# Attention operands of a head pair split when the pair's first head begins, with zero-padded low parts, another order in block 1 and other figures in the planner

## The chip, the core and the metric

The kernel runs on one core of a Trainium2 chip. The metric is the device time of one execution in microseconds. TensorE multiplies; VectorE (DVE), ScalarE (ACT) and GpSimd (POOL) do the elementwise work; the queue of SyncE (SP) carries most of the loads from device memory.

## The reference, cut to what matters

Three model blocks run one after the other on one sequence of 512 tokens of width 1024, all in float32:

```
x = first_block(x, c, ctx, c_ctx, ...)   # gated linear attention (4 heads) + depthwise conv (31 taps)
                                         # + spatial gating unit, three gates, then a feed-forward
x = second_block(x, ...)                 # 2 layers: feed-forward, hybrid mixer, feed-forward
x = third_block(x, c_3, ...)             # linear recurrence + block attention of 8 heads
```

Three things in it matter here. In block 1 the output is `gates0*y_a + gates1*y_b + gates2*y_c`, where `y_a` is the product of the gated linear attention (GLA), `y_b` that of the convolution and `y_c` that of the spatial gating unit, and every gate is a sigmoid of a projection of the same input. In each layer of block 2 the mixer has 8 softmax heads with a forget bias ("Fox", 64 features, in 4 pairs) and 4 differential heads ("Diff") of two 64-feature softmaxes each:

```
s_f = einsum('bhqd,bhkd->bhqk', qf, k_f) * scale + cf[..., None] - cum[..., None, :]
s_d = einsum('bhcqd,bhckd->bhcqk', qd, k_d) * scale
```

Block 3 has 8 causal softmax heads of 64 features (for 512 tokens its block selection keeps every past block), again in 4 pairs ("Moba").

## The kernel before

All large products run in a rounded float32 format with both operands split in a high and a low part, as three matmuls (`mm3`): weight high by input high, weight high by input low, weight low by input high. 24 of them (8 blocks of the contraction by 3) are a "unit" of 128 output columns by 512 tokens. Weights come as a stream of [128,1024] pieces, three in flight: SP loads `wraw`, ACT casts it to `whi`, and DVE (or POOL, for every second piece where `poolprep` is set) subtracts to get `wlo`.

Everything else is written as generators ("tasks") that are advanced after each `mm3` (`main_mm3`, then `tick`). The order of instructions on every engine is thus made when the program is built, by a planner: `Clock` adds up a cost for each instruction (`cost_pe`, `cost_act`, `cost_dve`, `cost_pool`), and `yield from k.sync()` holds a task back until the planned time of TensorE has reached the planned end of what the task waits for. On the chip TensorE takes its instructions in that order; where a planned time was too short, it waits. `room(n)` holds a task until n of the 78 [128,512] blocks of on-chip memory are free, and `idle()` advances the planner with no main matmul.

Attention works on pairs of heads of 64 features. `stack` makes the operands of a pair from a block `t` with both heads: for each head `e` of the queries a block `out[e]` with the high part on the head's own 64 partitions and the low part on the other 64; for the keys a block with the high part on both halves, and one block `low` for both heads that holds the low parts. `attn_scores` then makes each block of 128 queries by two matmuls: one over all 128 partitions (high and low query by high key), and one over the head's own 64 partitions (high query by low key). Three parts of a head (`PARTS`) cover its four query blocks: 512 key columns, 384, and two times 256.

Fox: `fox(j)` projects queries and keys of pair j, and starts a task `prep` for each that runs `stack` at once; a head is `ready` when both are stacked. Moba: `head_norms` ends with `stack` for each pair, all four of the queries ahead of the keys. Diff heads run `stack` in their own `prelude`, as they begin. At most four heads are live at a time (`HEADS`, `H3`), in the order in which they were started. The mixer ends in `out_proj`: a first pass over the Diff results, and a second one that needs the Fox results.

Block 1 begins with 8 loads of `x`, 8 of the first group of modulation weights (`ada.load(0)`), 3 weight pieces and 8 more of group 1, all on SP. `warm(7)` runs matmuls on zeros; sums of squares, `rms_cols` (row norms), `ada.rows(0)` and two calls of `prepare` follow, and then the first main matmuls. Later the units follow `ORDER_1`: "r" are gates of the GLA output, "g" the gates of a branch, "p" a product with a branch's output, which waits until all 8 blocks of that output are there, "a" starts the modulation rest, "v" and "s" belong to the spatial gating unit. The convolution (`conv_work`, 240 fused multiply-adds on DVE) is a filler that is advanced when DVE's planned queue is short.

Of the kernel before, what the change touches and what calls it, by code (L numbers as in the profile page):

```python
# [18 lines left out]
S = 512  # L19
SC = 256  # L20
KT = 8
# [202 lines left out]
def cost_dve(op, out, a, kw):  # L224
    n = width(out)
    if op == "reciprocal":
        return 0.07 + 6.4e-3 * n
    if op in ("tensor_scalar", "memset"):
        return max(0.2, 0.1 + 0.7e-3 * n)
    return max(0.2, 0.08 + 1.05e-3 * n)  # L230


def cost_pool(op, out, a, kw):
    return 0.06 + (1.0e-3 if op == "memset" else 2.3e-3) * width(out)


class Engine:
# [532 lines left out]
def stack(k, t, keys):  # L770


    nc = k.nc
    yield from k.sync()
    yield from k.room(4)
    out = [k.rblk(), k.rblk()]
    low = k.rblk() if keys else None
    own = [slice(0, 64), slice(64, 128)]
    for e in range(2):
        nc.scalar.copy(out[e].r[own[e]], t.f[own[e]])  # L780
    if keys:
        for e in range(2):
            nc.scalar.copy(out[e].r[own[1 - e]], t.f[own[e]])
    yield from k.sync()
    for e in range(2):
        lo = (low.r if keys else out[e].r)[own[e] if keys else own[1 - e]]
        nc.gpsimd.tensor_sub(lo, t.f[own[e]], out[e].f[own[e]])
    k.free(t)
    if keys:
        out.append(low)  # L790
    return out


def attn_scores(k, q, kk, e, part):
    b = k.bank()
    rows = slice(64 * e, 64 * e + 64)
    for qb, o in part:
        n, c = max((qb + 1) * P, 256), slice(qb * P, qb * P + P)
        k.nc.tensor.matmul(b[:, o:o + n], lhsT=q[e].r[:, c], rhs=kk[e].r[:, 0:n], start=True, stop=False)
        k.nc.tensor.matmul(b[:, o:o + n], lhsT=q[e].r[rows, c], rhs=kk[2].r[rows, 0:n], start=False, stop=True)  # L800
    return b


# [88 lines left out]
class Pair:  # L892

    nb = 1
    whole = True

    def turned(self, i):

# [89 lines left out]
class Fox(Pair):  # L988
# [8 lines left out]

    def prelude(self):
        k, nc, st = self.k, self.k.nc, self.st
        self.q, self.kk, self.v = st["q"][self.j], st["k"][self.j], st["v"]  # L1000
        yield from k.room(4)
        self.ncum, self.nmd, self.sm = k.blk(), k.blk(), k.tiny()
        b = yield from k.gbank()
        sel = k.negr[0:40, self.h:self.h + 1].to_broadcast([40, P])
        nc.tensor.matmul(b, lhsT=sel, rhs=st["cum"].r[0:40], start=True, stop=True)
        yield from k.sync()
        nc.scalar.copy(self.ncum.f, b)
        k.unbank(b)
        tri = k.c("mask")[:, None, 384:512].to_broadcast([P, 4, P])
        v = lambda ap: ap.rearrange("p (b q) -> p b q", q=P)  # L1010
        nc.gpsimd.tensor_add(v(self.nmd.f), v(self.ncum.f), tri)
# [170 lines left out]
def mixer2(k, layer, norm, start, add, done):  # L1182
    nc = k.nc
    w = "w_in_2"
    xs = norm.xs
    st = dict(q={}, k={}, dq={}, dk={}, t={}, o={}, do={}, done=[0] * 4, ddone=[])
    st["nlam"], st["subln"] = k.lam[layer]
    k.poolprep = True
    pf = k.bank()
# [46 lines left out]
            k.free(cosr)  # L1236
        k.start(attn_head(k, Diff(k, st, h), HEADS))

    def prep(name, j, t):
        yield from k.sync()  # L1240
        st[name][j] = yield from stack(k, t, name == "k")

    def fox(j):
        for name, base, s in (("q", FQ, 0.125), ("k", FK, 1.0)):
            b = k.bank()
            k.unit(b, w, layer, base + j * P, xs)
            t = k.blk()
            nc.vector.scalar_tensor_tensor(t.f, b, s, norm.bc, op0=ALU.mult, op1=ALU.mult)
            k.unbank(b)
            k.start(prep(name, j, t))  # L1250
        for e in range(2):
            k.start(attn_head(k, Fox(k, st, j, e), HEADS))

# [326 lines left out]
class Moba(Pair):  # L1580
# [6 lines left out]
        return self.j in self.st["ga"] and self.j in self.st["q"] and self.j in self.st["k"]  # L1587

    def prelude(self):
        self.q, self.kk = self.st["q"][self.j], self.st["k"][self.j]  # L1590
        self.sm = self.k.tiny()
        self.k.clk.t = self.k.clk.now + 1.0
        yield from self.k.sync()

    def reduce(self, qb, o, bs, ss):
        n = qb * P + P
# [6 lines left out]
def head_norms(k, banks, g, keys, dst):  # L1603

    nc = k.nc
    heads = lambda ap: ap.rearrange("p (h d) -> p h d", d=64)
    yield from k.sync()
    ts = []
    for b in banks:
        yield from k.room(2)  # L1610
        ts.append(k.blk())
        nc.scalar.copy(ts[-1].f, b)
        k.unbank(b)
        yield
    st = k.blk()
    v, y, u = (st.f[:, 32 * i:32 * i + 32] for i in range(3))
    yield from k.sync()
    for i, t in enumerate(ts):
        yield from k.room(2)
        sq = k.blk()  # L1620
        k.act(sq.f, t.f, AF.Square)
        yield from k.sync()
        nc.vector.tensor_reduce(out=v[:, 8 * i:8 * i + 8], in_=heads(sq.f), axis=mybir.AxisListType.X, op=ALU.add)
        k.free(sq)
    nc.vector.tensor_scalar(v, v, 1.0 / 64, EPS1, op0=ALU.mult, op1=ALU.add)
    k.rsqrt(y, v, u)
    for i, t in enumerate(ts):
        eng = nc.gpsimd if i % 2 else nc.vector
        eng.tensor_mul(heads(t.f), heads(t.f), y[:, 8 * i:8 * i + 8, None].to_broadcast([P, 8, 64]))
    k.free(st)  # L1630
    yield from k.sync()

    def pair(j):
        yield from k.wait(2)
        yield from k.room(3)
        b = k.bank()
        for i, t in enumerate(ts):
            nc.tensor.transpose(b[:, i * P:i * P + P], t.f[:, j * P:j * P + P], k.ident)
        yield from k.sync()
        t = k.blk()  # L1640
        k.act(t.f, b, AF.Copy, scale=g)
        k.unbank(b)
        yield from k.sync()
        dst[j] = yield from stack(k, t, keys)
    for j in range(4):
        k.start(pair(j))
        yield
    while len(dst) < 4:
        yield
    k.free(ts)  # L1650
# [78 lines left out]
def block3(k, x, norm, out):  # L1729
    nc = k.nc  # L1730
    w = "w_in_3"
    st = dict(q={}, k={}, t={}, o={}, ga={}, done=[0] * 4)
    k.poolprep = True
    bs = k.nbanks(4)
    for t, p in enumerate(norm.each()):
# [133 lines left out]
def between(b, ahead):  # L1869

    o = []
    for m in range(KT):
        o += some("p", [m], b)
        if m + ahead < KT:
# [1 line left out]
    return o  # L1876


ORDER_1 = (some("r", range(KT)) + some("g", range(6), 1) + some("g", range(6), 0) + between(1, 6) + some("a", [0])
           + between(0, 6) + some("v", range(2)) + some("s", range(KT)) + some("g", range(6), 2) + between(2, 6))  # L1880


def plan1():
# [75 lines left out]
class Ada1:  # L1959
# [20 lines left out]
    def rows(self, q):  # L1980

        k, nc = self.k, self.k.nc
        b, row = k.bank(), k.blk()
        for t in range(KT):
            nc.tensor.matmul(b[0:2], lhsT=self.sc[:, t, :], rhs=self.ws[q][t].f, start=t == 0, stop=t == KT - 1)
        nc.scalar.copy(row.f[0:2], b[0:2])
        k.unbank(b)
        b = k.bank()
        for i in range(4):
            nc.tensor.transpose(b[:, 2 * i:2 * i + 2], row.f[0:2, i * P:i * P + P], k.ident[0:2, 0:2])  # L1990
        for c in range(2):
            self.finish(q, c, b[:, c:8:2])
        k.unbank(b)
        k.free(row, self.ws.pop(q))

    def step(self, q, c, t, acc):
        ve, w, s = self.k.nc.vector, self.ws[q][t].f, self.sc[:, t, c:c + 1]
# [91 lines left out]
def gla_dir(k, st, h, s, res):  # L2089
# [48 lines left out]
                         start=True, stop=True)  # L2138
    pairs = lambda ap: ap.rearrange("p (b c t) -> p b c t", c=2, t=64)
    chunk = dec.rearrange("p (b c) -> p b c", c=2)  # L2140
    nc.gpsimd.tensor_mul(both, chunk[:, :, 0], chunk[:, :, 1])
    f, l = pairs(kd.f)[:, :, s], pairs(qe.f)[:, :, 1 - s]
    nc.gpsimd.tensor_mul(f, f, chunk[:, :, 1 - s:2 - s].to_broadcast([P, 4, 64]))
    nc.gpsimd.tensor_mul(l, l, chunk[:, :, s:s + 1].to_broadcast([P, 4, 64]))
# [284 lines left out]
def block1(k, x, nxt):  # L2429
    nc = k.nc  # L2430
    w = "w_in"
    st = dict(q={}, k={}, v={}, r={}, o={}, ck={}, cv={}, s0=[k.blk() for _ in range(4)], cdone=0, hdone=0,
              conv={}, hc={}, yb={}, z={}, sv={})
    for m in range(KT):
        x.append(k.blk())
        nc.sync.dma_start(x[m].f, k.a["x"][:, m, :])
    ada = Ada1(k)
    ada.load(0)
    k.w_start()
    ada.load(1)  # L2440
    warm(k, 7)
    k.clk.t = k.clk.c["dve"] = k.clk.c["act"] = 6.0
    acc = sumsq(k, [x[m].f for m in range(KT)], S, nc.vector)
    lt, ly = rms_cols(k, acc.f, S, EPS1)
    ada.rows(0)
    bcb = bc_rows(k, ly)
    hx = []

# [7 lines left out]
        k.free(x[m])  # L2456

    prepare(0)
    k.w_ensure(1)
    k.w_finish(1)  # L2460
    prepare(1)
    ada.load(2)
    cols = k.bank()
# [4 lines left out]
    for m in range(KT):  # L2468
        q = m // 2 + 1
        if m % 2 == 0 and q < 4:  # L2470
            k.fresh()
            for t in range(KT):
                ada.step(q, 0, t, gacc)
            summed = k.clk.t
        for n, c0 in enumerate(first_units()):
            k.main_mm3(fb[n], k.wnext(w, 0, m, c0), (hx[m][0].r, hx[m][1].r), m == 0, m == KT - 1)
            if m % 2 == 1 and n == 1 and q < 4:
                k.clk.t = summed
                ada.sums(cols[:, 4 * q:4 * q + 4], gacc)
                ada.finish(q, 0, cols[:, 4 * q:4 * q + 4])  # L2480
                for i in range(2):
                    prepare(m + 1 + i)
        if m == 0:
            ada.load(3)
        elif m == 2:
            for i in range(4):
                nc.scalar.dma_start(cq[i].f.rearrange("p (m t) -> p m t", t=SC), k.a["ctx"][:, 2 * i:2 * i + 2, :])
# [338 lines left out]
```

## Time and profile before

| what | value |
|---|---|
| time, median of 3 runs | 3515.91 us (3515.6 to 3515.91) |
| the profiled execution's own time | 3511.07 us |
| its span, first to last instruction | 3509.3 us |
| busy TensorE | 3405.3 us, 97% of the span |
| busy DVE / ACT / POOL | 1911.7 / 1351.7 / 720.5 us |
| mean granted TensorE clock | 0.98 |

The profiled execution is 1.8 us longer than its span and 4.8 us shorter than the median of the runs. A matmul counts as busy from its start to its modelled end, and the next one starts before that end; how long matmuls take in a row is therefore read from the starts of successive rows, not from the durations. In shapes, `128*128 128x512` are weights of 128 partitions by 128 columns and a moving operand of 128 partitions by 512 columns; `64*128` are weights on 64 partitions.

### The profile page before, as it was taken

Reading aid. Unit: us, or ns where it says so; the run is one execution under the profiler, and the core shown is the slowest. Engines: PE = TensorE matmul, PEld = TensorE weight load, DVE = VectorE, ACT = ScalarE, POOL = GpSimd, SP = SyncE. Lnnn points to the kernel's source line nnn. Section 1 sums busy time; section 2 is a strip of 40 time slices with the busy share of each in tenths; the row PEclk is TensorE's granted clock in tenths of the full one; section 3 lists DMA queues with packets and bytes.
Section 4 is the critical chain, followed back from the end, with each engine's and each line's share of the span. In section 5 each row is a group of like instructions: output and inputs, shape, how many; then the busy total and the mean of one; then the engine's idle time right before and its main releaser. Section 6 shows DMA issues by size and latency. Waiting matters only on the chain.

```text
span 3509.3 us, 39437 instructions
## 1 busy us (share of the span) xinstructions
PE 3405.3 (97%) x15210; PEld 2763.3 (79%) x15210; DVE 1911.7 (54%) x3010; ACT 1351.7 (39%) x2176; POOL 720.5 (21%) x564
## 2 busy tenths in 40 slices
PE   7998889999999999999999999999999999999999
PEld 5886678887888888887778888888887778888777
DVE  5899865655333365433686443344335774433566
ACT  3324462223322332324764222233227653232474
POOL 0004231222000101103452110011016331111362
PEclk9998999999999999999999999999999999999999
DMA  6211114543322244232122222322332123222221
GB/s 209 93 56 55 48 49 149 181 156 102 102 98 99 99 159 164 97 117 98 55 68 80 99 97 96 96 96 97 107 108 72 60 68 108 96 96 96 72 79 55
DMA packets 110189, 344.99 MB, mean 98 GB/s; under 512 B 13425, under 2 KB 13681, under 8 KB 110001
## 3 DMA queue, kind: packets, MB, share of 16 engines
q1 hardware_dynamic: 84960, 296.78, 25.2%
q10 hardware_dynamic: 23760, 41.50, 3.7%
q0 software_dynamic: 1280, 4.20, 0.4%
q8 instruction: 119, 1.95, 0.2%
q14 instruction: 70, 0.57, 0.1%
HBM read 336.13 MB, written 6.29 MB: 98 GB/s over the span
## 4 chain that ended last, share of the span: by engine, by line
PE 52%; DVE 4%; ACT 2%; POOL 1%; issue 1%; DVEq 0%; POOLq 0%; ACTq 0%
PE bk L256 52%; DVE b L256 3%; ACT b L256 1%; DVE tinies L256 1%; POOL b L256 1%; POOL wlo L256 0%; DVE wlo L256 0%; ACT whi L256 0%; ACT L251 0%; ACT bk L256 0%; ACT tinies L256 0%; DVE small L256 0%; DVEq L256 0%; POOLq L256 0%; ACTq L256 0%
## 5 line engine op out<-in xcount | busy, mean ns | idle before, releaser
L256 PE MATMUL bk<-b,whi 128*128 128x512 f32 (+1 forms) x8048 | 2514.7, 394 | 6.8 <-ACT whi L256 3.4
L256 PEld LDWEIGHTS bk<-b,whi 128*128 128x128 f32 x8048 | 1506.7, 190 | 323.3 <-issue 9.6
L256 PE MATMUL bk<-b,wlo 128*128 128x512 f32 (+1 forms) x4024 | 1575.4, 391 | 6.7 <-DVE wlo L256 5.9
L256 POOL TENSOR_TENSOR b<-b,b 128x512 f32<-128x512 f32 (+2 forms) x381 | 528.4, 1395 | 2391.1 <-DVE b L256 1189.4
L256 DVE TENSOR_TENSOR wlo<-wraw,whi 128x1024 fp32r<-128x1024 f32 x495 | 643.8, 1303 | 528.8 <-ACT whi L256 528.5
L256 PEld LDWEIGHTS bk<-b,wlo 128*128 128x128 f32 x4024 | 762.2, 189 | 170.1 <-DVE wlo L256 8.8
L256 ACT CAST whi<-wraw 128x1024 fp32r<-128x1024 f32 x542 | 568.0, 1049 | 739.8 <-PE bk L256 442.8
L256 ACT CAST b<-b 128x512 fp32r<-128x512 f32 (+3 forms) x286 | 176.0, 618 | 523.9 <-POOL b L256 369.9
L256 DVE TENSOR_TENSOR b<-bk,b 128x512 f32<-128x512 f32 (+6 forms) x324 | 208.1, 659 | 253.7 <-PE bk L256 212.9
L256 DVE TENSOR_TENSOR b<-b,b 128x512 fp32r<-128x512 f32 (+3 forms) x250 | 184.7, 745 | 251.0 <-ACT b L256 248.9
L256 PE MATMUL bk<-b,b 128*128 128x128 f32 (+9 forms) x1056 | 250.4, 354 | 33.2 <-POOL b L256 20.4
L256 ACT ACTIVATE b<-b 128x512 f32<-128x512 f32 (+1 forms) x259 | 153.4, 608 | 308.7 <-DVE b L256 273.1
L256 PEld LDWEIGHTS bk<-b,b 128*128 128x128 f32 (+3 forms) x1056 | 174.1, 193 | 109.9 <-issue 36.0
L256 PE MATMUL bk<-whi,b 128*128 128x512 f32 x768 | 248.4, 397 | 4.0 <-ACT b L256 2.2
L256 DVE SCALAR_TENSOR_TENSOR b<-b,pvt,b 128x392 f32<-128x392 f32 (+7 forms) x296 | 229.0, 778 | 33.3 <-ACT b L256 26.4
L256 PEld LDWEIGHTS bk<-whi,b 128*128 128x128 f32 x768 | 145.6, 190 | 36.6 <-DVE b L256 3.0
L256 DVE SCALAR_TENSOR_TENSOR b<-b,small,b 128x512 f32<-128x512 f32 (+1 forms) x178 | 148.0, 833 | 20.8 <-ACT b L256 15.5
L256 POOL TENSOR_TENSOR wlo<-wraw,whi 128x1024 fp32r<-128x1024 f32 x47 | 116.0, 2467 | 202.3 <-ACT whi L256 175.7
L256 PE MATMUL bk<-wlo,b 128*128 128x512 f32 x384 | 150.8, 393 | 0.0
L256 PE MATMUL bk<-cst,b 128*128 128x128 f32 (+1 forms) x776 | 111.5, 271 | 36.3 <-DVE b L256 25.3
L256 PEld LDWEIGHTS bk<-cst,b 128*128 128x128 f32 x776 | 98.9, 168 | 60.4 <-DVE b L256 31.8
L256 ACT ACTIVATE b<-bk 128x512 f32<-128x512 f32 (+2 forms) x170 | 97.2, 572 | 111.6 <-PE bk L256 109.9
(93 smaller groups left out, 1233.9 us busy)
## 6 DMA issues: line engine op xcount, KB each, us to landing
wraw<-in_wst SPq DMA_DIRECT2D x542, 512.0 KB, 3.3
b<-in_ada1r ACTq DMA_DIRECT2D x64, 256.0 KB, 4.4
b<-in_ada ACTq DMA_DIRECT2D x48, 256.0 KB, 4.1
b<-in_ada SPq DMA_DIRECT2D x32, 256.0 KB, 5.5
xpark<-b ACTq DMA_DIRECT2D x16, 256.0 KB, 2.0
b<-xpark POOLq DMA_DIRECT2D x16, 256.0 KB, 5.2
b<-in_x SPq DMA_DIRECT2D x8, 256.0 KB, 5.2
b<-in_x ACTq DMA_DIRECT2D x8, 256.0 KB, 4.5
```

What stands on the lines that cost most here:

```text
L256: return f(*a, **kw)
```

## The change

`stack` makes one low block for each head of the keys, and ACT writes zeros (copied from a zero column of `mask`) to the half of it that is not the head's own. The second matmul of `attn_scores` runs over all 128 partitions. Fox and Moba keep `t`, and the pair's first head stacks queries and keys in its `prelude`; the second head waits for that. In block 1 the order of the start, `ORDER_1` and the engine of one small product are changed, and three planner costs.

```diff
 def cost_dve:
+    if op == "tensor_tensor_scan":
+        return 0.03 + 2.2e-3 * n
+    if op == "scalar_tensor_tensor" and n > 300 and len(tuple(out.shape)) == 3:
+        return 0.2 + 1.1e-3 * n
 def cost_pool:
-    return 0.06 + (1.0e-3 if op == "memset" else 2.3e-3) * width(out)
+    return 0.06 + 1.0e-3 * width(out) if op == "memset" else max(0.5, 0.1 + 2.7e-3 * width(out))
 def stack:
-    yield from k.room(4)
+    yield from k.room(5 if keys else 4)
-    low = k.rblk() if keys else None
+    lows = [k.rblk(), k.rblk()] if keys else out
...
             nc.scalar.copy(out[e].r[own[1 - e]], t.f[own[e]])
+            nc.scalar.copy(lows[e].r[own[1 - e]], k.c("mask")[own[1 - e], 0:1].to_broadcast([64, S]))
...
-        lo = (low.r if keys else out[e].r)[own[e] if keys else own[1 - e]]
-        nc.gpsimd.tensor_sub(lo, t.f[own[e]], out[e].f[own[e]])
+        nc.gpsimd.tensor_sub(lows[e].r[own[e] if keys else own[1 - e]], t.f[own[e]], out[e].f[own[e]])
 def attn_scores:
-        k.nc.tensor.matmul(b[:, o:o + n], lhsT=q[e].r[rows, c], rhs=kk[2].r[rows, 0:n], start=False, stop=True)
+        k.nc.tensor.matmul(b[:, o:o + n], lhsT=q[e].r[:, c], rhs=kk[2 + e].r[:, 0:n], start=False, stop=True)
 class Pair:
+    def stacks(self):
+        k, st, j = self.k, self.st, self.j
+        if j not in st["stk"]:
+            st["stk"][j] = None
+            qk = {}
+            def part(name):
+                qk[name] = yield from stack(k, st[name][j], name == "k")
+            yield from both_of(k, [part("q"), part("k")])
+            st["stk"][j] = qk["q"], qk["k"]
+        while st["stk"][j] is None:
+            yield
+        self.q, self.kk = st["stk"][j]
 Fox.prelude:
+        yield from self.stacks()
 fox(j):
-            k.start(prep(name, j, t))
+            st[name][j] = t
 Moba.prelude:
-        self.k.clk.t = self.k.clk.now + 1.0
-        yield from self.k.sync()
+        yield from self.stacks()
 head_norms:
-        dst[j] = yield from stack(k, t, keys)
+        dst[j] = t
-ORDER_1 = (some("r", range(KT)) + some("g", range(6), 1) + some("g", range(6), 0) + between(1, 6) + some("a", [0])
-           + between(0, 6) + some("v", range(2)) + some("s", range(KT)) + some("g", range(6), 2) + between(2, 6))
+ORDER_1 = (some("r", range(KT)) + some("g", range(KT), 0) + some("g", range(KT), 1) + some("a", [0]) + between(0, KT)
+           + between(1, KT) + some("v", range(2)) + some("s", range(KT)) + some("g", range(6), 2) + between(2, 6))
 gla_dir:
-    nc.gpsimd.tensor_mul(both, chunk[:, :, 0], chunk[:, :, 1])
+    nc.vector.tensor_mul(both, chunk[:, :, 0], chunk[:, :, 1])
 block1:
+    ada = Ada1(k)
+    ada.load(0)
     for m in range(KT):
         x.append(k.blk())
         nc.sync.dma_start(x[m].f, k.a["x"][:, m, :])
-    ada = Ada1(k)
-    ada.load(0)
+    k.w_start(1)
+    ada.load(1)
     k.w_start()
-    ada.load(1)
-    warm(k, 7)
+    row = ada.rows(0)
+    warm(k, 3)
...
-    ada.rows(0)
+    ada.turn(0, row)
+    k.w_ensure(0)
+    k.w_finish(0)
+    warm(k, 3)
     bcb = bc_rows(k, ly)
...
     prepare(0)
-    k.w_ensure(1)
-    k.w_finish(1)
     prepare(1)
...
-            if m % 2 == 1 and n == 1 and q < 4:
+            if m % 2 == 1 and n == 3 and q < 4:
```

`ada.rows` is cut in two: `rows` runs the matmuls, and the new `turn` copies, transposes and finishes. With `between(0, KT)` the eight products of a branch follow one another with no gate unit among them.

## Rows read from the trace of the kernel before

**Rows 1.** Stretches: from:to, length, busy (instructions) of PE, PEld, DVE, ACT, POOL; PEclk, DMA

```profile
1100.00:1150.00 50.00, 50.00 (x222) 41.40 (x221) 18.00 (x17) 14.65 (x18) 2.58 (x2) 1.00 0.28 95
263.00:508.00 245.00, 204.68 (x947) 164.72 (x948) 211.76 (x293) 127.16 (x248) 94.75 (x83) 0.90 0.15 50
1650.00:1863.00 213.00, 206.16 (x903) 152.28 (x902) 155.71 (x420) 143.78 (x333) 106.92 (x88) 0.95 0.19 65
2660.00:2874.00 214.00, 208.28 (x922) 155.36 (x922) 157.15 (x421) 141.98 (x333) 107.81 (x89) 0.96 0.20 66
3390.00:3483.00 93.00, 87.89 (x400) 65.34 (x399) 63.98 (x171) 63.29 (x133) 33.73 (x35) 0.96 0.14 46
```

**Rows 2.** TensorE's groups by shape: count, busy us, mean ns, idle before, releasers

```profile
L256 PE MATMUL bk<-b,b 64*128 64x256 f32 x80 | 31.9, 398 | 0.0
L256 PE MATMUL bk<-b,b 64*128 64x512 f32 x40 | 20.1, 503 | 8.4 <-POOL b L256 8.4
L256 PE MATMUL bk<-b,b 64*128 64x384 f32 x40 | 18.8, 470 | 0.0
```

**Rows 3.** Timeline of TensorE in Diff heads: start, length, operation, count; scores are `bk<-b,b`

```profile
1722.02 2.55 PE L256 MATMUL bk<-b,b 128*128 128x256 f32 x8
1724.50 0.50 PE L256 MATMUL bk<-whi,b 128*128 128x512 f32 x1
1724.84 0.39 PE L256 MATMUL bk<-wlo,b 128*128 128x512 f32 x1
...
1728.39 1.67 PE L256 MATMUL bk<-b,b 128*128 128x512 f32 x4
1729.99 0.50 PE L256 MATMUL bk<-whi,b 128*128 128x512 f32 x1
```

**Rows 4.** Groups by shape on ACT and POOL: `stack`'s casts and subtractions, `gla_dir`'s `both`

```profile
L256 ACT CAST b<-b 64x512 fp32r<-64x512 f32 x120 | 74.0, 616 | 4.1 <-POOL b L256 1.9 <-DVE b L256 0.2
...
L256 POOL TENSOR_TENSOR b<-b,b 64x512 fp32r<-64x512 f32 x80 | 109.6, 1370 | 43.1 <-ACT b L256 36.3 <-issue 2.0
...
L256 POOL TENSOR_TENSOR tinies<-tinies 128x4 f32<-128x4 f32 x8 | 5.6, 705 | 0.0
```

**Rows 5.** Timeline of TensorE where block 3's first Moba head begins

```profile
3396.78 0.79 PE L256 MATMUL bk<-b,b 64*128 64x512 f32 x1 [4.88 <-POOL b L256]
```

**Rows 6.** TensorE's waits from 263 to 508 us: total us, times, longest

```profile
PE bk L256 <- POOL b L256: 19.3, 10, 3.3
PE bk L256 <- DVE b L256: 16.9, 4, 7.9
```

**Rows 7.** Timelines of POOL and DVE: three taps beside POOL's five operations, four later

```profile
336.92 8.30 POOL L256 TENSOR_TENSOR b<-b,b 128x512 f32<-128x512 f32 x5 [7.78 <-DVE b L256]
...
342.35 5.04 DVE L256 SCALAR_TENSOR_TENSOR b<-b,pvt,b 128x480 f32<-128x480 f32 x3
...
370.89 2.70 DVE L256 SCALAR_TENSOR_TENSOR b<-b,pvt,b 128x424 f32<-128x424 f32 x4
```

**Rows 8.** TensorE's main groups to 519.5 us, and GLA's last transposes (timeline)

```profile
L256 PE MATMUL bk<-b,whi 128*128 128x512 f32 (+1 forms) x830 | 264.6, 403 | 3.4 <-ACT whi L256 3.4
...
L256 PE MATMUL bk<-whi,b 128*128 128x512 f32 x192 | 59.4, 389 | 0.0
...
519.57 0.60 PE L256 MATMUL bk<-cst,b 128*128 128x128 f32 x4
```

**Rows 9.** Timeline of the start

```profile
6.61 4.26 ACT L256 ACTIVATE b<-b 128x512 f32<-128x512 f32 x8
...
7.40 8.56 PE L256 MATMUL bk<-b 128*128 128x512 f32 x14 [7.40 <-DVE b L256]
...
16.67 7.03 PE L256 MATMUL bk<-b,small 128*2 128x512 f32 x16
...
29.26 1.22 PE L256 MATMUL bk<-b,whi 128*128 128x512 f32 x2 [3.41 <-ACT whi L256]
...
40.59 1.87 PE L256 MATMUL bk<-cst,b 128*128 128x1 f32 x8 [3.84 <-DVE b L256]
```

More of the change, by code (lines that the diff above doesn't have):

```diff
@@ L783, in stack @@
             nc.scalar.copy(out[e].r[own[1 - e]], t.f[own[e]])
+            nc.scalar.copy(lows[e].r[own[1 - e]], k.c("mask")[own[1 - e], 0:1].to_broadcast([64, S]))
     yield from k.sync()
     for e in range(2):
-        lo = (low.r if keys else out[e].r)[own[e] if keys else own[1 - e]]
-        nc.gpsimd.tensor_sub(lo, t.f[own[e]], out[e].f[own[e]])
+        nc.gpsimd.tensor_sub(lows[e].r[own[e] if keys else own[1 - e]], t.f[own[e]], out[e].f[own[e]])
     k.free(t)
-    if keys:
-        out.append(low)
-    return out
+    return out + lows if keys else out
 def attn_scores(k, q, kk, e, part):
     b = k.bank()
-    rows = slice(64 * e, 64 * e + 64)
     for qb, o in part:
@@ L999, in prelude @@
         k, nc, st = self.k, self.k.nc, self.st
-        self.q, self.kk, self.v = st["q"][self.j], st["k"][self.j], st["v"]
+        self.v = st["v"]
+        yield from self.stacks()
         yield from k.room(4)
@@ L1185, in mixer2 @@
     xs = norm.xs
-    st = dict(q={}, k={}, dq={}, dk={}, t={}, o={}, do={}, done=[0] * 4, ddone=[])
+    st = dict(q={}, k={}, stk={}, dq={}, dk={}, t={}, o={}, do={}, done=[0] * 4, ddone=[])
     st["nlam"], st["subln"] = k.lam[layer]
@@ L1237, in diff @@
         k.start(attn_head(k, Diff(k, st, h), HEADS))
-    def prep(name, j, t):
-        yield from k.sync()
-        st[name][j] = yield from stack(k, t, name == "k")
     def fox(j):
@@ L1589, in prelude @@
     def prelude(self):
-        self.q, self.kk = self.st["q"][self.j], self.st["k"][self.j]
         self.sm = self.k.tiny()
-        self.k.clk.t = self.k.clk.now + 1.0
-        yield from self.k.sync()
+        yield from self.stacks()
     def reduce(self, qb, o, bs, ss):
@@ L1731, in block3 @@
     w = "w_in_3"
-    st = dict(q={}, k={}, t={}, o={}, ga={}, done=[0] * 4)
+    st = dict(q={}, k={}, stk={}, t={}, o={}, ga={}, done=[0] * 4)
     k.poolprep = True
@@ L1982, in rows, with turn @@
         k, nc = self.k, self.k.nc
-        b, row = k.bank(), k.blk()
+        b = k.bank()
         for t in range(KT):
             nc.tensor.matmul(b[0:2], lhsT=self.sc[:, t, :], rhs=self.ws[q][t].f, start=t == 0, stop=t == KT - 1)
+        k.free(self.ws.pop(q))
+        return b
+    def turn(self, q, b):
+        k, nc = self.k, self.k.nc
+        row = k.blk()
         nc.scalar.copy(row.f[0:2], b[0:2])
@@ L1993, in rows @@
         k.unbank(b)
-        k.free(row, self.ws.pop(q))
+        k.free(row)
     def step(self, q, c, t, acc):
```

## The prediction

> **What bounds the kernel now.** I read the busy times by stretch first [rows 1]. A stretch in which only the dense products run, 1100 to 1150 us, is 100% TensorE at the full clock, with 222 matmuls of 512 columns: 0.225 us each. DVE is busy for 18 us of the 50 there, ACT for 15. Such stretches are TensorE's own time, and nothing in the diff touches them. What can move lies in four other stretches. From 263 to 508 us (block 1, GLA beside the convolution) TensorE is busy for 204.7 of 245 us at a mean clock of 0.90: 40.3 us idle, and 245 x 0.10 = 24.5 us given to the lower clock level (1.2 instead of 2.4 GHz), 65 us together. In the two mixers of block 2 and in block 3's attention it is idle for 6.8, 5.7 and 5.1 us and gives 10.7, 8.6 and 3.7 us to the clock, 41 us in all, so it bounds these 520 us too. The reader should see that DVE is at 73% in the mixers and at 86% in block 1, so there the other engines are close behind.
>
> Then I asked what TensorE does in the attention, by shape and in order of time. The score matmuls over 64 partitions are 80 + 40 + 40 = 160 [rows 2]. In the timeline a group of eight score matmuls of 256 columns, four over 128 partitions alternating with four over 64, takes from 1722.02 to 1724.50, 2.48 us [rows 3]. At the dense rate, half of 0.225 us each, it would be 0.90. The next matmul takes 0.34 us to the one after it, 0.115 too long. So the group costs 1.58 + 0.115 = 1.70 us more than its columns, 0.42 for each pair of matmuls. The four of 512 columns take 1.60 us where 0.90 would do; with the same 0.115 that is 0.41 a pair. No engine is waited for in these rows: the cost sits in the change between the two row heights.
>
> **The padded score matmul.** It has as many columns as before and reads 128 partitions, as the first of its pair does. The rows show what a matmul costs whose weights have the height of the one ahead: 0.225 us at 512 columns [rows 1]. So I take the whole 0.40 us a pair (a little under both groups, since some groups are followed by another attention matmul): 160 x 0.40 = 64 us of TensorE. Bounds: nothing (the weight load of the second matmul shows up whatever its height) and 160 x 0.42 = 67 us.
>
> The Trainium skill (TensorE: Matmul & The Clock Gate, Part 3, "The mechanism") says that a weight load overlaps a matmul in flight only where their row groups differ. By that rule two full-height matmuls in a row would overlap no load, the padding would save nothing, and 64 in the sum would be 0. The trace disagrees: 222 full-height matmuls, each with its own weights, run in 50 us.
>
> **What the padding and the later stack add.** Twenty key stacks (8 Fox, 8 Diff, 4 Moba) each get two casts of a [64,512] half on ACT, at 0.616 us [rows 4]: 40 x 0.616 = 25 us of ACT. In a mixer 9.9 us come on top of 143.8 in 213. That work is hidden beside TensorE except ahead of a first Diff head, where it may sit on the way: 2 x 1.2 us, counted among the waits below.
>
> For the 12 Fox and Moba pairs the stack moves: 2 + 4 + 2 casts on ACT (4.9 us) and 4 subtractions on POOL (4 x 1.37 = 5.5 us) now start when a head has become live. No DMA moves with it. Casts and subtractions overlap, so some 8 us. Behind them queue ACT's weight casts, the exponentials of the live heads and POOL's weight halves; the stream's three pieces (3 x 5.4 us of units of 24 matmuls) cover the weights. What covers the head itself is the dense units that TensorE still has, and the two other live heads. If that cover is gone, each round of two pairs costs up to 8 us.
>
> With 64 us taken out of TensorE, the other engines come nearer. A mixer loses 64 of 160 score pairs x 0.40 = 25.6 us: DVE goes from 155.7/213 = 73% to 155.7/187 = 83%, ACT from 68% to 153.7/187 = 82%; block 3 loses 12.8 us, DVE goes from 69% to 80%. None becomes the bound, but waits grow. The trace of before has no such mixer, so I bound the new loss by nothing and the whole 64, and choose near the rows of the attention, not those of block 1 where DVE is at 86%: the 41 us lost there now grow by half, 20 us. Against that, block 3's first head now waits for 4.88 us [rows 5] on POOL, which makes queries' and keys' stacks for all pairs first; now pair 0 has its own, minus 4. Attention: 64 - 20 + 4 = 48 us gained.
>
> **Block 1.** TensorE's waits there are for POOL and DVE [rows 6], 36 of the 40 us. Two things in the diff speak to them. The planner's cost for a tap of the convolution was 0.08 + 1.05e-3 x 480 = 0.58 us, now 0.73. Without POOL four taps take 2.70 us, 0.67 each; beside POOL's operations three take 5.04, 1.68 each [rows 7]. So DVE ran behind its plan, GLA's operations queued behind taps, and TensorE stood at GLA's matmuls. The new figure fits the tap alone and still misses the one beside POOL. Second, eight [128,4] products of 0.705 us [rows 4] go from POOL to DVE: at most 5.6 us of GLA's chain.
>
> The order moves the first product with GLA's output from behind 30 units to behind 24, 6 x 5.4 = 32 us earlier, and that of the convolution from behind 20 to behind 32, 65 us later. Is GLA ready? Its last transposes stand at 519.57 us, behind (830 + 192)/2 = 511 main triples [rows 8]. By the code 496 triples precede the first product, so GLA ends 15 triples, two units, into the products: two units inside the new limit. The convolution gets 12 units more. So I expect the order to hold and the waits to go down, not away: half of 65, 32 us. Bounds: nothing, and 65.
>
> **The start.** The 8 loads of `x` now stand behind 8 of the modulation weights. ACT's squares follow the landing of `x` from 6.61 to 10.87 [rows 9], about 0.55 us each, so they end some 5 us later; the 7.03 us of row matmuls, which came after 8.56 us of warm-up, come first. The first main matmul, at 29.26, then hangs on the norm, three warm-ups behind it and `prepare`; I find it within 2 us of where it was, with TensorE kept busy until then. Sums at n = 3 wait two units' share less for DVE (3.84 us at 40.59), but leave as much less cover for the `prepare` behind them. Zero; bounds 4 us either way.
>
> **The sum.** 48 + 32 + 0 = 80 us off the profiled execution's own 3511.1: 3431. The median of the runs stands 4.8 us above that execution: 3436 us.
>
> **Rivals.** All from the median, 3515.9.
>
> *The attention becomes a chain.* Two rounds of Fox pairs in a mixer each show their 8 us, and so do Moba's two: 6 x 8 = 48 us, which leaves nothing of the attention's gain; part of the first round is covered by units, so 40 us lost. 3515.9 - 8 - 32 = 3476. For it: DVE and ACT at 82%, and no more than four heads at a time. Against it: TensorE now has hardly a wait in the mixers. 0.15.
>
> *Block 1 gains nothing*, because a tap beside POOL still takes 1.68 us against a planned 0.73, and GLA is wanted 32 us earlier. 3515.9 - 48 = 3468. 0.17.
>
> *The padding doesn't do what it says*: the second load stays in sight. Then the attention's new waits stay away too, and 32 + 4 remain: 3480. Against it stands every dense stretch. 0.05. This is the case that the skill's rule above would make.
>
> *Slower:* the blocks run out. Sixteen gate blocks are held before the first product, where 12 were; if GLA's tasks are held back for room until the units are used up, its second half, 415 to 520 us, runs with few dense matmuls beside it, and some 95 us of the 105 are lost: 3515.9 + 95 - 48 = 3563. It turns the sign when over 48 us of GLA are left at the 24th unit. Against it: r blocks and the heads' q and k blocks come free as GLA goes on. 0.03.
>
> *Better:* all 64 + 4 of the attention and most of block 1, 56: 3392. 0.10.
>
> **How the numbers follow.** The forecast has the remaining 0.50, and its own range is 3410 to 3464 (attention 37 to 60, block 1 15 to 46). The range that leaves out no more than 2 in 10 runs from 3400, halfway to the better case, to 3482, past the padding case. About 0.2% (7 us) can be told from no change. Faster: 0.50 + 0.15 + 0.17 + 0.05 + 0.10 = 0.97, less 0.02 for two of the bad cases at once; same 0.02; slower 0.03.
>
> **What would show it.** No shape of 64 partitions left on TensorE; groups of score matmuls at their columns' rate (eight of 256 columns in 0.9 us, not 2.5); 160 casts of [64,512] on ACT. The mixers' stretches some 20 us shorter each, with idle time of TensorE no more than doubled. In block 1 the waits for POOL and DVE halved, and no long wait at the first product of branch 0. I am wrong if TensorE's gaps in the mixers pile up ahead of score matmuls on POOL or ACT (the chain), or if the padded matmuls keep the 0.31 us of their neighbours.

## The result, and the profile after

| what | before | after |
|---|---|---|
| median of the runs | 3515.88 us | 3471.76 us (3471.05 to 3473.23) |
| after / before | | 0.9875 (95%: 0.9858 to 0.9892) |
| span of the profiled execution | 3509.3 us | 3471.5 us |
| busy TensorE / DVE / ACT / POOL | 3405.3 / 1911.7 / 1351.7 / 720.5 us | 3348.1 / 1915.9 / 1373.7 / 718.9 us |

The kernel became 44 us faster by the medians, where 80 were forecast; between the two profiled executions it is 37.8 us, and the places below add up to that. Both kernels issue the same 13,224 main matmuls (weights from `whi` or `wlo`), so a stretch can be measured from the start of the Nth to the start of the Mth in both. All runs stand in this table, in us; block 1 begins with the units of `r`, block 3 with its first main matmul, and the count ends at the start of the last one, 4.2 us before the end in every run. Each row is one execution (those of the kernel before took 3505 to 3525 us as a whole), so differences of a few us in one row prove nothing:

```
kernel         to r   block 1  mixer 0  mixer 1  block 3  the rest
before         271.4   592.9    284.3    281.2    238.9    1836.3
after          274.6   567.5    273.4    283.2    233.5    1835.1
late_only      270.4   592.8    286.7    281.6    240.2    1837.0
pad_only       272.7   592.8    274.9    271.5    236.8    1836.7
ahead          277.1   565.4    273.6    279.9    238.7    1837.0
spread         276.9   565.5    277.6    271.7    234.7    1835.2
costs          273.6   565.7    286.5    281.5    239.1    1833.1
pe_less        273.5   568.5    272.3    277.1    234.6    1834.4
dve_less       274.5   566.9    259.5    274.1    233.1    1835.9
heads5         272.4   566.2    273.2    281.7    233.1    1838.0
old_order      273.4   596.6    273.8    283.4    233.6    1835.7
old_costs      277.8   593.0    275.5    268.1    233.7    1837.1
start_before   269.0   566.8    274.0    284.7    233.7    1835.7
lighter        269.5   565.7    275.9    275.8    233.7    1835.7
```

So 3.2 us were lost in the start, 25.4 gained in block 1, 10.9 in mixer 0, nothing in mixer 1 (2.0 lost; kernels with the same work there scatter by 17 us, as shown below), 5.4 in block 3. The attention, which was to give 48 us, gave 14.

**The padding did what was forecast.** The timeline of TensorE in Diff heads of the kernel after (start, length, operation, count):

```profile
1700.55 1.07 PE L260 MATMUL bk<-b,b 128*128 128x512 f32 x4
1701.46 0.62 PE L260 MATMUL bk<-b,whi 128*128 128x512 f32 x2
...
1720.28 1.11 PE L260 MATMUL bk<-b,b 128*128 128x256 f32 x8
1721.23 0.63 PE L260 MATMUL bk<-b,whi 128*128 128x512 f32 x2
```

From start to next start, four score matmuls of 512 columns take 0.91 us and eight of 256 take 0.95, against 1.60 and 2.48 in [rows 3]. With the 0.115 us of the matmul behind the group that is (1.60 - 0.91 + 0.115) / 2 = 0.40 and (2.48 - 0.95 + 0.115) / 4 = 0.41 us a pair: the 64 us left TensorE. None of the three shapes of [rows 2] is left. The rule of the Trainium skill that was weighed in the prediction (TensorE: Matmul & The Clock Gate, Part 3, "The mechanism", that a weight load overlaps only where row groups differ) does not agree with these rows either. ACT's new casts, groups by shape of the kernel after, come to the forecast 25 us:

```profile
L260 ACT CAST b<-b 64x512 fp32r<-64x512 f32 x120 | 74.1, 617 | 2.2
...
L260 ACT CAST b<-cst 64x512 fp32r<-64x512 f32 x40 | 24.7, 617 | 0.6
```

**Where it went.** Busy time by stretch (columns as in [rows 1]) of block 1 from `r` to the last unit ahead of the second branch, the two mixers, and block 3 from its queries and keys on; first the kernel before, then after:

```profile
271.00:575.00 304.00, 264.03 (x1204) 213.50 (x1204) 233.45 (x325) 153.11 (x287) 96.24 (x85) 0.92 0.19 64
1602.00:1886.00 284.00, 277.16 (x1224) 211.29 (x1223) 184.56 (x458) 175.20 (x377) 135.34 (x104) 0.96 0.20 68
2610.00:2892.00 282.00, 276.28 (x1229) 211.46 (x1227) 189.06 (x461) 173.46 (x376) 132.08 (x103) 0.97 0.21 69
3364.00:3509.00 145.00, 135.63 (x624) 104.33 (x622) 91.39 (x212) 90.63 (x174) 58.98 (x48) 0.98 0.17 59
```

```profile
275.00:557.00 282.00, 258.47 (x1210) 210.12 (x1209) 244.03 (x352) 153.55 (x291) 91.73 (x76) 0.95 0.22 74
1579.00:1852.00 273.00, 252.74 (x1224) 208.56 (x1223) 186.72 (x456) 183.06 (x395) 134.83 (x103) 0.96 0.21 71
2576.00:2860.00 284.00, 258.75 (x1229) 212.74 (x1227) 188.56 (x460) 183.95 (x393) 133.97 (x103) 0.94 0.21 68
3331.00:3471.00 140.00, 127.22 (x623) 104.93 (x621) 93.31 (x220) 92.03 (x180) 56.55 (x47) 0.96 0.17 59
```

Length less busy TensorE is its idle time: in the last three stretches 6.8 + 5.7 + 9.4 = 22 us before and 20.3 + 25.2 + 12.8 = 58 after, 36 more. Length times what the clock lacks of 1 is an estimate of what the lower level cost: 11.4 + 8.5 + 2.9 = 23 before, 10.9 + 17.0 + 5.6 = 34 after, 11 more. New waits and the lower clock took 47 of the 64 us, where the prediction had 20 for both. TensorE's waits in mixer 1, before and after (total us, times, longest):

```profile
PE bk L256 <- DVE b L256: 4.1, 3, 2.6
PE bk L256 <- POOL b L256: 1.6, 2, 1.3
```

```profile
PE bk L260 <- DVE b L260: 15.6, 11, 2.9
PE bk L260 <- DVE tinies L260: 5.1, 2, 4.9
PE bk L260 <- DVE wlo L260: 4.6, 2, 2.4
```

All of the new waiting in mixer 1 is for DVE, which is busy for the same 189 us in both. In mixer 0 the waits for DVE rose from 4.6 to 17.4 us. The chain of work that ended last in mixer 1, from the end of the Diff heads' projections on, says it by shares; before, then after:

```profile
by line: PE bk L256 74.3%; DVE b L256 13.1%; DVE tinies L256 8.2%; ACT b L256 2.5%; DVE wlo L256 1.2%; issue 1.0%; ACT whi L256 0.5%; ACT bk L256 0.2%
```

```profile
by line: PE bk L260 49.2%; DVE b L260 31.5%; DVE tinies L260 9.8%; ACT b L260 5.4%; DVE wlo L260 2.5%; issue 2.2%; ACT bk L260 0.4%; DVEq L260 0.1%
```

TensorE's share fell from 74 to 49%, DVE's rose from 13.1 + 8.2 + 1.2 = 22% to 44%. The chain also changes hands more often: it has 121 pieces in 192 us before and 311 in 205 us after. (In mixer 0 TensorE fell from 57 to 38% and DVE rose from 34 to 45%.) Block 3 differs. The same shares for its last two rows above, before and after:

```profile
by line: PE bk L256 82.8%; POOL wlo L256 3.9%; POOL b L256 3.5%; ACT b L256 3.4%; DVE b L256 3.1%; ACT whi L256 0.6%; issue 0.5%; DVE tinies L256 0.3%; DVEq L256 0.0%; POOLq L256 0.0%
```

```profile
by line: PE bk L260 52.1%; ACT b L260 18.6%; issue 9.5%; DVE b L260 6.7%; POOL wlo L260 3.4%; POOL b L260 3.1%; ACT whi L260 2.2%; ACT L255 1.0%; POOLq L2841 0.9%; DVE tinies L260 0.6%; ACTq L260 0.0%
```

There ACT's `b` went from 3.4 to 18.6%, among it the sixteen casts of two late stacks, from 3359 to 3369 us. Most of that is hidden beside TensorE's dense units; behind it TensorE waits for POOL for 2.25 us, at 3377.6 us. DVE holds 7%.

**The start.** The timeline of ACT and of TensorE, after, to set against [rows 9]:

```profile
10.74 5.37 ACT L260 ACTIVATE b<-b 128x512 f32<-128x512 f32 x8 [4.86 <-DMA b<-in_x]
```

```profile
5.94 8.53 PE L260 MATMUL bk<-b,small 128*2 128x512 f32 x16 [5.94 <-ACT small L260]
14.40 2.84 PE L260 MATMUL bk<-b 128*128 128x512 f32 x6
...
23.40 5.49 PE L260 MATMUL bk<-b 128*128 128x512 f32 x6 [4.31 <-DVE b L260]
...
31.75 0.49 PE L260 MATMUL bk<-b,whi 128*128 128x512 f32 x1 [1.63 <-ACT b L260]
```

The squares end at 16.1 us, not 10.9, as forecast; TensorE stands still for 4.31 us ahead of the second warm-up, and the first main matmul starts 2.5 us later.

### The profile page after: what moved, and what is told of

It reads as the page before. It is cut to its first block, busy times and chain, and to the rows that moved or that the text cites. A ratio compares the mean times of both kernels' runs of the same rounds, so it can differ in the third digit from the quotient of the medians.

```text
span 3471.5 us, 39465 instructions
## 1 busy us (share of the span) xinstructions
PE 3348.1 (96%) x15208; PEld 2757.0 (79%) x15208; DVE 1915.9 (55%) x3016; ACT 1373.7 (40%) x2220; POOL 718.9 (21%) x556
## 4 chain that ended last, share of the span: by engine, by line
PE 48%; DVE 6%; ACT 3%; issue 1%; POOL 1%; POOLq 0%; DVEq 0%; ACTq 0%
PE bk L260 48%; DVE b L260 4%; ACT b L260 3%; DVE tinies L260 1%; DVE wlo L260 0%; ACT whi L260 0%; POOL b L260 0%; POOL wlo L260 0%; ACT L255 0%; POOLq L2841 0%; ACT bk L260 0%; ACT tinies L260 0%; DVEq L260 0%; DVE small L260 0%; ACTq L260 0%
## 5 line engine op out<-in xcount | busy, mean ns | idle before, releaser
L260 DVE SCALAR_TENSOR_TENSOR b<-b,pvt,b 128x392 f32<-128x392 f32 (+7 forms) x296 | 237.3, 806 | 33.0 <-ACT b L260 26.4
L260 PE MATMUL bk<-b,b 128*128 128x256 f32 (+6 forms) x1056 | 205.7, 337 | 28.3 <-DVE tinies L260 8.5
L260 PEld LDWEIGHTS bk<-b,b 128*128 128x128 f32 (+2 forms) x1056 | 171.9, 201 | 60.9 <-POOL b L260 17.4
```

What stands on the lines that cost most here:

```text
L260: return f(*a, **kw)
```

## The experiments

Three theories were open for the attention. *Late stack* is the prediction's rival of a chain: the moved `stack` holds each head up. *Plan*: the planner prices DVE and ACT too low here; slow score matmuls had hidden that. *Load*, formed after `costs`: DVE's amount of work now sets the end, whatever the plan says. Each ratio is to runs of the kernel before on the same chip, whose median there was 3515.2 to 3518.2 us.

**Padding alone, and the stack's place alone.** `pad_only` is the kernel before with the new `stack` and `attn_scores`; `late_only` has the new `stacks` and no padding; `ahead` is the kernel after with the stacks made ahead (Fox's line; the same is done for Moba):

```diff
-            st[name][j] = t
+            k.start(prep(name, j, t))
```

Expected of `pad_only`: 

> The kernel before, with the two low blocks, their zeros and the full-height second score matmul, and nothing else of the change: stacks are still made ahead. The late-stack theory (a pair's eight casts come in one piece on ACT as its first head begins, ahead of the exponentials of the live heads) expects nearly all of the 64 us of TensorE back: some 3460 us. Its rival, the plan theory (ACT's and DVE's planned costs are too short, and the slow score matmuls gave them the time they lacked), expects only what the changed kernel kept in its attention, some 14 us: 3500 us.

Of `late_only`: 

> The kernel before with the stacks made by the pair's first head, with no padding and nothing else. Late-stack theory: the bursts on ACT cost here too, though the slow score matmuls hide part: 3520 to 3540 us. Plan theory: no change, 3516 us within 7.

Of `ahead`: 

> The changed kernel with the stacks made ahead again in Fox and Moba, as before, but padded. Late-stack theory: the mixers and block 3 lose their new waits, 35 us or so, 3437 us. Plan theory: the waits stay, 3472 us within 8.

Measured: `pad_only` 3491.0 us (0.993, 0.9915 to 0.9946), `late_only` 3517.9 (1.001, 0.9998 to 1.0021), `ahead` 3476.4 (0.9887, 0.9867 to 0.9906). The late stack falls twice: by itself it costs nothing, and taken out again it gives nothing. Padding alone gives 24 us of its 64, so the new waits come with the padding and need nothing else of the change.

**The stack's casts apart.** `spread` lets each cast wait until ACT is less than 0.6 us ahead of TensorE in the plan (one of its three places):

```diff
+        yield from k.calm("act", 0.6)
         nc.scalar.copy(out[e].r[own[e]], t.f[own[e]])
```

Expected: 

> The changed kernel with the stack's casts held apart in the plan, each waiting until ACT's planned queue is under 0.6 us, so that other heads' exponentials come between them; the stacks are as late as in the changed kernel or later. If the burst is what costs: some 20 us faster, 3450 us. If the lateness itself costs: 3472 us or slower. Plan theory: 3472 us within 8.

Measured: 3466.8 us (0.9864, 0.9847 to 0.9881). The interval overlaps that of the kernel after; a burst that costs 20 us is excluded, one of 5 is not.

**The plan's prices.** `costs` fits them to the trace, from block 2 on:

```diff
+    if FIT[0]:
+        return 0.16 + 0.86e-3 * width(out) + (0.3 if kw.get("accum_out") is not None else 0.0)
     return 0.08 + 0.9e-3 * width(out)
...
+    if FIT[0]:
+        return max(0.2, (0.24 if op == "tensor_tensor_reduce" else 0.15) + 1.05e-3 * n)
     return max(0.2, 0.08 + 1.05e-3 * n)
```

Expected: 

> The changed kernel, with the planner's costs from block 2 on set to what the trace shows: an ACT operation 0.16 us + 0.86 ns an element, 0.3 more when it also accumulates; a DVE operation 0.15 us + 1.05 ns an element, 0.24 for a multiply that also accumulates. The plan theory (saved TensorE time became waiting, because DVE and ACT fall behind a plan that prices them too low) expects 20 to 30 us off the changed kernel's 3472, near 3445, all of it in the two mixers and block 3. If the waits come from the load itself (DVE and ACT have so much work per score group, whatever the plan says), the time stays within 7 us of 3472, or rises, since a longer price also puts work off.

Measured: 3487.2 us (0.9911, 0.9898 to 0.9925), 15 us slower than the change. The plan theory as it stood falls. Its mixer 0 shows why, in busy time by stretch up to the second pass of the output projection and from there on:

```profile
1576.00:1794.00 218.00, 206.64 (x995) 170.97 (x994) 143.03 (x348) 143.55 (x306) 116.32 (x79) 0.98 0.26 84
1794.00:1862.00 68.00, 54.16 (x231) 41.25 (x230) 44.66 (x115) 40.02 (x86) 22.55 (x25) 0.85 0.05 16
```

With dearer prices TensorE goes ahead with dense units instead of waiting, and is 11 us idle in the first 218; then the units are gone and 45 us of DVE's work are left, beside which it stands 14 us idle at a clock of 0.85. The waiting was moved, not removed, which speaks against an order that a better plan would mend.

**TensorE's work or DVE's.** `pe_less` leaves out the second score matmul, that is the low part of the keys' product; `dve_less` leaves out the normalizing multiply of Fox and Moba:

```diff
-        k.nc.tensor.matmul(b[:, o:o + n], lhsT=q[e].r[:, c], rhs=kk[e].r[:, 0:n], start=True, stop=False)
-        k.nc.tensor.matmul(b[:, o:o + n], lhsT=q[e].r[:, c], rhs=kk[2 + e].r[:, 0:n], start=False, stop=True)
+        k.nc.tensor.matmul(b[:, o:o + n], lhsT=q[e].r[:, c], rhs=kk[e].r[:, 0:n], start=True, stop=True)
```

```diff
-        for qb, o in part:
-            v = ss[0].f[:, o:o + qb * P + P]
-            ve.tensor_scalar(v, v, self.sm.f[:, 16 + qb:17 + qb], None, op0=ALU.mult)
```

Expected of `pe_less`: 

> The changed kernel without the second score matmul, so the output lacks the low part of the keys' product: 160 matmuls of 512, 384 and 256 columns, at 0.225 us for 512 some 25 us less of TensorE. If TensorE bounds the attention, near 3447. If DVE's chain of work sets the end, TensorE only waits longer: 3465 to 3472.

Of `dve_less`: 

> The changed kernel without the multiply that normalizes the rows of Fox and Moba (32 operations on DVE, 17.2 us, in each mixer and as many in block 3: 52 us in all); the output lacks that factor. If DVE's work is now part of what sets the end of the attention, a good part of the 52 us comes back: by DVE's 41% of the chain that ends last in the second mixer, 21 us, near 3451; up to 40 us if DVE alone sets it. If TensorE bounds the attention still, or if only the order of issue is at fault, the time stays within 7 us of 3472.

Measured: `pe_less` 3466.4 us (0.986, 0.9843 to 0.9876), `dve_less` 3449.6 (0.9808, 0.9794 to 0.9823). 25 us off TensorE gave 5, which the intervals hardly tell from nothing; 52 us off DVE gave 22. By the table the 22 come from the mixers (13.9 and 9.1 for 17 us of DVE each); block 3, where DVE holds 7% of the chain, gave 0.4 for its 17. The 13.9 are clear of the scatter (but for `costs`, all full kernels with the new score matmuls lie between 273.2 and 277.6 us in mixer 0); the 9.1, and what `pe_less` shows in the mixers, are not. The same chain of mixer 1, without DVE's multiply and then without TensorE's matmul:

```profile
by line: PE bk L260 58.6%; DVE b L260 18.0%; ACT b L260 10.7%; DVE tinies L260 9.5%; issue 2.1%; DVE wlo L260 1.7%; ACT bk L260 0.4%; DVEq L260 0.0%
```

```profile
by line: PE bk L260 36.3%; DVE b L260 32.0%; DVE tinies L260 11.8%; ACT b L260 11.5%; DVE wlo L260 4.0%; issue 3.4%; ACT whi L260 1.5%; DVEq L260 0.1%; ACTq L260 0.0%
```

DVE's share goes to 29% in the one and to 48% in the other. Without DVE's multiply the chain goes to TensorE (59%) and ACT (11%); without TensorE's matmul it goes to ACT (5 to 13%) and DVE. What these two runs show is that DVE's operations in a head cost time and that TensorE's hardly do. They don't show that it is DVE's *amount* of work: the multiply is also a step on every head's own way from scores to products, so leaving it out shortens that way too. In mixer 0 `pe_less` reaches its second pass 23 us sooner than the kernel after (at 1804 and at 1826 us) and ends it at 1852, as that does; the stretch between is

```profile
1804.00:1852.00 48.00, 38.45 (x166) 29.62 (x164) 34.64 (x76) 23.37 (x47) 10.73 (x10) 0.86 0.07 24
```

**More heads at a time.** `heads5` has `HEADS = 5`. Expected: 

> The changed kernel with five heads live at a time in the mixers instead of four (block 3 is not touched). If the waits are latency (four chains too few to keep DVE and TensorE busy), 10 to 20 us less: 3452 to 3462. If DVE's amount of work sets the end, or blocks and banks hold the fifth head back, within 7 us of 3472.

Measured: 3470.5 us (0.9868, 0.9853 to 0.9883): no difference. The fifth head was not kept out: the matmul with `negr`, which a Fox head does ahead of its scores, comes for the second Fox head at 1718.2 us instead of 1734.2, and for the sixth of mixer 1 at 2768.9 instead of 2789.1. So some heads did begin sooner, and that didn't fill the waits.

**Block 1: order or prices.** `old_order` and `old_costs` put one of the two back:

```diff
-ORDER_1 = (some("r", range(KT)) + some("g", range(KT), 0) + some("g", range(KT), 1) + some("a", [0]) + between(0, KT)
+ORDER_1 = (some("r", range(KT)) + some("g", range(6), 1) + some("g", range(6), 0) + between(1, 6) + some("a", [0])
```

```diff
-    if op == "tensor_tensor_scan":
-        return 0.03 + 2.2e-3 * n
-    if op == "scalar_tensor_tensor" and n > 300 and len(tuple(out.shape)) == 3:
-        return 0.2 + 1.1e-3 * n
```

`old_costs` has POOL's old price as well. Expected of `old_order`: 

> The changed kernel, with block 1's order of the kernel before. Block 1 gave back 26 us of TensorE's time. If the order earned it, the time is near 3498; if the new planner's costs did, it stays near 3472. The prediction's step (costs right the waits, the order merely holds) expects at most 10 us more: 3472 to 3482.

Of `old_costs`: 

> The changed kernel, with the three planner's costs of the kernel before (scan, tap of the convolution, POOL). The prediction's step puts most of block 1's 26 us here: 3490 to 3498. If the order earned it, 3472. Since the costs also hold in blocks 2 and 3, the stretches there are looked at by themselves: no change expected, within 5 us.

Measured: `old_order` 3502.6 us (0.9954, 0.9942 to 0.9967), `old_costs` 3488.1 (0.9909, 0.9896 to 0.9923). In block 1 each loses all that was gained (596.6 and 593.0 us, 592.9 before, 567.5 after): neither half is worth anything alone. Both keep the eight products that moved from POOL to DVE, so these gain nothing by themselves either. TensorE's waits in the stretch of 282 us shown above and its counterpart in `old_costs`:

```profile
PE bk L260 <- POOL b L260: 8.9, 5, 3.4
PE bk L260 <- ACT b L260: 7.8, 2, 7.4
...
PE bk L260 <- DVE b L260: 1.0, 2, 0.9
```

```profile
PE bk L256 <- POOL b L256: 17.6, 10, 3.9
PE bk L256 <- DVE b L256: 15.2, 6, 8.3
PE bk L256 <- ACT b L256: 4.2, 2, 3.9
```

With the old prices the waits are those of [rows 6], whatever the order. With the new prices and the old order the waits for POOL are the 8.9 us of the kernel after, but those for ACT are 16.3 and those for DVE's `b` 8.8. From 489 to 517 us TensorE's timeline shows these, where the kernel after waits no longer than 0.9 us:

```profile
490.10 2.08 PE L260 MATMUL bk<-b,b 128*128 128x256 f32 x4 [3.64 <-DVE b L260]
...
497.84 2.43 PE L260 MATMUL bk<-cst,b 128*128 128x128 f32 x8 [5.66 <-ACT b L260]
...
507.39 2.07 PE L260 MATMUL bk<-cst,tinies 128*128 128x128 f32 x8 [4.47 <-DVE tinies L260]
...
512.36 0.80 PE L260 MATMUL bk<-b,whi 128*128 128x512 f32 x1 [2.90 <-ACT b L260]
...
515.68 0.80 PE L260 MATMUL bk<-b,whi 128*128 128x512 f32 x1 [2.52 <-DVE b L260]
```

The last two are dense matmuls that wait for their operand `b`. `old_costs` also took 15 us less in mixer 1, where no change was expected: prices of a few operations reshuffle its plan. Nine kernels with the same work there lie between 268 and 285 us, 278 in the mean, so a single difference below some 17 us in mixer 1 proves nothing. That holds for the 2.0 us lost there by the change, too: the mean of the nine is 3 us below the kernel before.

**The start.** `start_before` puts the start of the kernel before into the kernel after. Expected: 

> The changed kernel, with the start of block 1 of the kernel before (loads of x first, seven warm-up matmuls, row matmuls behind the norm, sums at the second unit). The start of the changed kernel takes 4.5 us longer to the first 144 main matmuls: if that is carried to the end, 3467; if block 1 waits for GLA and the convolution anyway, 3472.

Measured: 3465.6 us (0.9852, 0.9838 to 0.9865), 6 us less by the medians, with intervals that overlap. The table tells more: `r` begins at 272.4 to 277.8 us in the nine kernels with the new start, 274.9 in the mean, and at 269.0 to 272.7 in the five with the old one (`lighter`, below, among them), 270.6 in the mean. The new start costs some 4 us.

**Less of DVE's work, same output.** `lighter` is `start_before` with more of the weights' low halves on POOL:

```diff
-            eng = nc.gpsimd if self.poolprep and i % 2 else nc.vector
+            eng = nc.gpsimd if self.poolprep and i % 3 else nc.vector
```

Expected: 

> The changed kernel with block 1's start of the kernel before, and two of three low halves of the weights made by POOL in blocks 2 and 3 where one of two was (a low half is 1.42 us of DVE or 2.49 us of POOL). Both parts leave the output as it is. The start alone measured 3465.6. By the rate that the run without the normalizing multiply shows (22 us gained for 52 us of DVE, 0.43), 6 low halves less on DVE in each mixer and some 4 in block 3, 16 x 1.42 = 23 us, give 10 us: 3456. If POOL's work slows DVE beside it or POOL's longer halves come late for TensorE, 3465 or more. If the amount of DVE's work is not what sets the attention's end, 3465.

Measured: 3461.6 us (0.9839, 0.9824 to 0.9854), the fastest median of a kernel with the full output, and its interval lies below that of the kernel after (0.9858 to 0.9892); 4 us below `start_before`, less than the forecast 10, and not told apart from it by the intervals. The load theory gets no support from this: by the table mixer 0 became 1.9 us longer, and the 8.9 us off mixer 1 are within the scatter. Groups of mixer 0, `start_before` and then `lighter`:

```profile
L260 DVE TENSOR_TENSOR wlo<-wraw,whi 128x1024 fp32r<-128x1024 f32 x15 | 20.7, 1382 | 12.1 <-ACT whi L260 11.6 <-POOL b L260 0.4
```

```profile
L260 DVE TENSOR_TENSOR wlo<-wraw,whi 128x1024 fp32r<-128x1024 f32 x10 | 15.3, 1534 | 5.4 <-ACT whi L260 5.4
```

DVE makes five low halves less, but each takes 1.53 us instead of 1.38, so 5.4 us leave it where 6.9 would. The Trainium skill warns of this (Perfetto Trace Analysis, "Optimizing Scalar/DVE Operations"): DVE and GpSimd share a read port, so moving work between the two may not help. The trace of `lighter` agrees: the three of these ten that begin during a low half on POOL take 1.84 to 2.61 us, those beside nothing 1.21 to 1.23.

## Why the prediction was right in sign and too large

- **The padded score matmul, 64 us: right**, 0.40 to 0.41 us a pair.
- **The casts, 25 us of ACT; the later stack, hidden: right**, but for the 2.25 us in block 3, a wait for POOL's part of a late stack at the first head of the second pair. `late_only` and `ahead` show nothing of the 8 us a round. That rival named 3476 us, close to the result by luck, for its mechanism isn't there.
- **The attention's new waits, 20 us: this step failed; they are 47.** The load was foreseen: DVE was to come to 83% of a mixer's later part and came to 161.9 of 205 us, 79%, in mixer 1. Wrong was the step from there: that an engine busy for 83% doesn't become the bound, and with it the choice of half more than the 41 us lost before. At this load DVE had 44% of the chain in mixer 1, and a microsecond less of it gave 22/52 = 0.43 (13.9/17 in mixer 0, nothing in block 3), one less of TensorE's 5/25 = 0.2, hardly told from nothing. The prediction's own sign, idle time in the mixers no more than doubled, failed: it went from 6.8 to 20.3 and from 5.7 to 25.2 us. The step read DVE's share as slack beside TensorE, as if their work were parallel; the chain, with 311 pieces where it had 121, goes back and forth between them. Whether DVE's amount of work, the length of a head's way through both engines, or POOL's holding up DVE (last section) makes the waits is open: no run here takes one of the three away alone.
- **Block 1, 32 us: 25**, within its bounds. Mechanism half right: the planner's prices halve the waits for POOL with either order (19.3 to 8.9 us), but those for DVE's `b` (16.9 us) go to 8.8 with the old order, with 16.3 new for ACT, and to 1.0 only with the new one. The order, taken only as a risk, is needed as much. The eight products moved from POOL to DVE gave nothing beside the old prices (593.0 us, with 17.6 of waits for POOL).
- **The start, 0 with bounds of 4 us: some 4 lost**, at the bound. The later squares were foreseen; but TensorE was not "kept busy until then": it waits 4.31 us ahead of the second warm-up.
- **Block 3's first head, 4 us:** the wait of [rows 5] is gone from there, but the 2.25 us at the second pair stand against it. Taking 17 us of DVE off there brought nothing, and DVE holds 7% of that chain; what ACT's part costs there was not tried.

By profile the terms were 64 - 47 = 17, seen as 14 in the table's lengths; 25 in block 1; minus 3 in the start; 1 elsewhere: 37.8 us. (The 3 us between 17 and 14 lie within the rounding of the clock, which is given to two places.) The other 6 between the medians come from the profiled execution of before, 4.8 us below its median, and that of after, 1.5 above.

## What to carry to other kernels

When work is taken from the engine that bounds a stretch, don't stop at the other engines' busy share: where work alternates between two engines, new waits for the second can take most of what is saved while it is 80% busy. Here new waits, in the mixers for DVE, and the lower clock took 47 of 64 us. Read its share of the chain that ended last, or take a known amount off each engine and compare what comes back. And two halves of a change may be worth something only together, as the order and the prices were here; undo them one by one before giving either the credit.

## What the runs showed that was not expected

A DVE operation on one column can take nine times as long beside POOL. From the timeline of DVE and POOL in mixer 1 after:

```profile
2719.79 0.22 DVE L260 SCALAR_TENSOR_TENSOR tinies<-tinies,small 128x1 f32<-128x1 f32 x1
...
2722.58 2.40 POOL L260 TENSOR_TENSOR wlo<-wraw,whi 128x1024 fp32r<-128x1024 f32 x1 [13.74 <-ACT whi L260]
...
2722.96 2.04 DVE L260 SCALAR_TENSOR_TENSOR tinies<-tinies,small 128x1 f32<-128x1 f32 x1
```

The same operation takes 0.22 us alone and 2.04 when POOL has begun a low half of the weights; it ends 0.02 us after POOL's. The sixteen of mixer 1 take 12.5 us, where 16 x 0.22 would be 3.5. The Trainium skill (SBUF — State Buffer, "SBUF: two separate sides") says that a DVE operation with two inputs in SBUF and a GpSimd operation that reads SBUF lock a shared port pair against each other for a whole instruction; these rows agree. Such rows sit on the path of every Diff head, and no run here took them off.

Other DVE operations show the same. In mixer 1 of the kernel after, 299 of DVE's operations begin while POOL has nothing running, and none of these takes over 0.1 us more than the fastest tenth of its kind and shape in the run. Of the 161 that begin during an operation of POOL, 39 do, by 39 us together; before the change it was 36, by 37 us. So part of what is counted above as DVE's busy time is an estimated 39 us of standing behind POOL, and some of what `dve_less` gained may be that.
